# A two-layer hybrid encoder on one core: unused bytes between SBUF tiles that set the operands' addresses modulo 128

## The chip, the cores and the metric

One core of a Trainium2 chip. TensorE multiplies matrices (PE in the profile, and PEld for its loads of the operand that stays in the array), VectorE (DVE), ScalarE (ACT) and GpSimd (POOL) do the rest, SyncE (SP) issues most transfers. The metric is device time in microseconds of one execution. Three executions of the kernel before took 2242.03, 2242.40 and 2243.55 us; the median is 2242.4.

## The reference

Two layers over x of 256 tokens by 2048. Each layer:

```
h = x @ w_in                                   # 2048 -> 4928 columns
a = MLA heads (8, low-rank q and kv, rotary, chunk-causal softmax)
r = retention heads (4, decay, GroupNorm, swish gate)
x = LayerNorm(ALPHA * x + concat(a, r) @ w_out)
x = LayerNorm(ALPHA * x + (silu(x @ w_gate) * (x @ w_up)) @ w_down)   # 5632 wide
```

All in float32; nearly all of the work is products of x or of something made from x with weights that are read from memory once.

## The kernel before

A float32 product is made of three fp32r products: each operand is split into a high part (`split`, ACT writes `hi`) and a rest (DVE writes `lo`), and every 128 deep step of a product issues hi with hi, lo with hi, hi with lo. Weights come as units of up to 128 x 2048 numbers: SP loads one into a tile `raw`, ACT and DVE split it into `hi` and `lo` (three buffers of each), TensorE uses it, and `W.done()` lets the unit three further on be prepared. The order of all this is the order in which the Python code records it; tile pools decide the addresses.

A matmul instruction has a stationary operand of 128 columns, which PEld loads into the array, and a moving operand that streams through it. Two helpers issue nearly all of them. `mm_x` (lines 231 to 238) and `mm` of `strassen_group` (lines 790 to 795) keep 128 tokens of the activations still and stream 512 (once 320) weight columns. `mm_w` (lines 240 to 245) keeps 128 weight columns still and streams all 256 tokens. Every matmul loads a new stationary operand, so there are as many loads as matmuls.

The stages of a layer, with the tiles they write in PSUM: `cq` and `ckv` (`mm_x` over `xTh`, `xTl`), `pg` (`mm_w`), `pqn`, `pr`, `pkn`, `pv` (the low-rank q and kv, from `cqTh`, `cqTl` and `ckT`), `prv` with attention between it, `prq` (`mm_w`, retention), `wo` (over `mixAh`, `mixRh` and their `l`), then the feed-forward in four parts: `gb` and `ub` or, for ten of eleven column blocks, a Strassen group (`sX`, `sQ`, `sW`, `sY`, `sZ`, `sR` over `xTh`, `xTl`, and over four sums of it in `sfh`, `sfl`), and after each part `db` (`mm_x` over `hTh`, `hTl` with `w_down`).

Where the tiles lie, as the built program has it (first byte within a partition, modulo 128; every slice that a matmul takes begins at a multiple of 512 bytes in its tile): `res`, `xTh`, `xTl` at 0. `ident`, `raw`, `hi`, `lo` at 96, since the pool `const` ends 96 bytes past a multiple of 128. `sfh`, `sfl`, `hTh`, `hTl` and the Strassen blocks' own `raw` (pool `rs`) at 32. Attention tiles (`cqTh`, `mixAh`, `mixRh`, ...) at 64, because the table `cst` of 1953 numbers ends 32 bytes off; in layer 0 the slots `rg`, `rv`, `s8` are laid out ahead of `cst` and lie at 32, so `ckT` is at 32 in layer 0 and at 64 in layer 1.

So the two operands of a matmul lie 0, 32 or 64 bytes apart modulo 128 (the shorter way round):

| kind | moving over stationary | columns | matmuls | before: moving, stationary | apart | after | apart |
|---|---|---|---|---|---|---|---|
| a | `hi`, `lo` over `xTh`, `xTl` | 512 | 3600 | 96, 0 | 32 | 64, 0 | 64 |
| b | `hi`, `lo` over `mixA`, `mixR`, `cqT`; `ckT` of layer 1 | 512 | 840 | 96, 64 | 32 | 64, 0 | 64 |
| c | `xTh`, `xTl` over `hi`, `lo` (`pg`, `prq`) | 256 | 2304 | 0, 96 | 32 | 0, 64 | 64 |
| d | `cqT`; `ckT` of layer 1, over `hi`, `lo` (`pqn`, `pkn`) | 256 | 240 | 64, 96 | 32 | 0, 64 | 64 |
| e | `hi`, `lo` over `xTh`, `xTl` (`ckv`) | 320 | 192 | 96, 0 | 32 | 64, 0 | 64 |
| f | `hi`, `lo` over `hTh`, `hTl`, `sfh`, `sfl`; `ckT` of layer 0 | 512 | 3096 | 96, 32 | 64 | 64, 0 | 64 |
| g | `ckT` of layer 0 over `hi`, `lo` (`pkn`) | 256 | 48 | 32, 96 | 64 | 0, 64 | 64 |
| h | transposes: `ident` over `v`, `sf`, `sg` | 128 | 208 | 96, 32 | 64 | 96, 0 | 32 |
| i | transposes: `ident` over the rest | 128 | 252 | 96, 0 or 64 | 32 | 96, 0 | 32 |
| k | float32 products of attention and retention, two passes each | 128, 256 | 304 | several | 0 or 32 | 0, 0 | 0 |

These are the 11084 matmuls of the trace.

Of the kernel before, what the change touches and what calls it, by code (L numbers as in the profile page):

```python
# [10 lines left out]
F32 = mybir.dt.float32  # L11
# [7 lines left out]
P = 128  # L19
# [17 lines left out]

C_DEC, C_MASK, C_INVR, C_INVM = 0, HR * 384, HR * 384 + 384, HR * 384 + 385
N_CONST = C_INVM + RD // 2
N_COLS = 4 + 2 + 8 + 8  # L40


# [68 lines left out]
def trunk(ctx: ExitStack, tc: tile.TileContext, x, pos, w, lnp, cols, eye, consts, out):  # L111
    nc = tc.nc
    V, A, PE, G = nc.vector, nc.scalar, nc.tensor, nc.gpsimd

    const = ctx.enter_context(tc.tile_pool(name="const", bufs=1))
# [7 lines left out]
    xTl = const.tile([P, KD, S], F32R, name="xTl")  # L123
    colt = const.tile([P, DEPTH * N_COLS], F32, name="colt")
    rtC = const.tile([P, 1, S], F32, name="rtC")
# [3 lines left out]
    mhalf = const.tile([P, 8], F32, name="mhalf")  # L129

    ident = const.tile([P, P], F32, name="ident")

    def bank(tag_name):
        return psp.tile([P, 512], F32, tag="ps", name=tag_name)
# [96 lines left out]
    def mm_x(ps, ncol, tok, unit, xh, xl, k0, nk, first, last):  # L231
        wh, wl = unit
        for k in range(nk):
            sh = xh[:, k0 + k, tok * P:(tok + 1) * P]
            sl = xl[:, k0 + k, tok * P:(tok + 1) * P]
            PE.matmul(ps[:, :ncol], sh, wh[:, k, :ncol], start=first and k == 0, stop=False)  # L236
            PE.matmul(ps[:, :ncol], sh, wl[:, k, :ncol], start=False, stop=False)  # L237
            PE.matmul(ps[:, :ncol], sl, wh[:, k, :ncol], start=False, stop=last and k == nk - 1)  # L238
# [76 lines left out]
    def chunk_tail(banks, nu, xh, xl, k0, fin):  # L315
        for u in range(nu - 3):
            (unit,) = W.get()
            for tok in range(2):
                mm_x(banks[tok], 512, tok, unit, xh, xl, k0 + 4 * u, 4, u == 0, False)
            W.done()  # L320
        units = W.get(3)
        for i in range(3):
            u = nu - 3 + i
            mm_x(banks[0], 512, 0, units[i], xh, xl, k0 + 4 * u, 4, u == 0, u == nu - 1)
        fin(0)
        for i in range(3):
            u = nu - 3 + i
            mm_x(banks[1], 512, 1, units[i], xh, xl, k0 + 4 * u, 4, u == 0, u == nu - 1)
            W.done()
            if i < 2:  # L330
                pop(1)
        fin(1)

    def ln_params(pool, tags, i):
        g = pool.tile([P, D], F32, tag=tags[0], name=f"lng{i}")
        b = pool.tile([P, D], F32, tag=tags[1], name=f"lnb{i}")
        nc.sync.dma_start(g, lnp[2 * i].partition_broadcast(P))
        nc.sync.dma_start(b, lnp[2 * i + 1].partition_broadcast(P))
        return g, b
# [1 line left out]
    V.memset(mhalf, -0.5)  # L341

    def att_consts():
        cst = att.tile([P, N_CONST], F32, tag="cst", name="cst")
        nc.sync.dma_start(cst, consts)
        krE = att.tile([P, S], F32, tag="krE", name="krE")
        krO = att.tile([P, S], F32, tag="krO", name="krO")
        V.memset(krE, 0.0)
        V.memset(krO, 0.0)
        return cst, krE, krO  # L350

    att_ctx = ExitStack()
    att = att_ctx.enter_context(tc.tile_pool(name="att0", bufs=1))
# [18 lines left out]
    nc.scalar.dma_start(posc, pos.rearrange("(t p) -> p t", p=P))  # L372
    nc.sync.dma_start(posr, pos.partition_broadcast(P))
    cst, krE, krO = att_consts()
    nc.sync.dma_start(colt, cols)
    norm = Norm("i")
# [38 lines left out]
    for l in range(DEPTH):  # L415
        col = colt[:, l * N_COLS:(l + 1) * N_COLS]
        if l:
            att_ctx = ExitStack()
            att = att_ctx.enter_context(tc.tile_pool(name=f"att{l}", bufs=1))
            cst, krE, krO = att_consts()  # L420
# [262 lines left out]
        def resid(banks, c, t, norm_, scale=ALPHA):  # L683
            y = res[:, t, 512 * c:512 * (c + 1)]
            V.scalar_tensor_tensor(y, y, scale, banks[t], ALU.mult, ALU.add)  # L685
            if norm_ is not None:
                norm_.stat(t, c)
# [45 lines left out]
        ffp = ff_ctx.enter_context(tc.tile_pool(name=f"ff{l}", bufs=1))  # L733
# [23 lines left out]
        def h_flush(hTh, hTl, f0):  # L757
            while hprev:
                t, c, hh = hprev.pop(0)
                pt = bank("pth")  # L760
                for j in range(4):
                    PE.transpose(pt[:, j * P:(j + 1) * P], hh[:, j * P:(j + 1) * P], ident)
                k0 = 4 * (c - f0)
                split(hTh[:, k0:k0 + 4, t * P:(t + 1) * P], hTl[:, k0:k0 + 4, t * P:(t + 1) * P],
                      pt.rearrange("p (j t) -> p j t", j=4))
# [17 lines left out]
        def strassen_group(c, flush):  # L783
# [74 lines left out]
            hprev.append((0, c, v2))  # L858
            hprev.append((1, c, v5))

        for f0, f1 in FF_PARTS:
            nk = 4 * (f1 - f0)
            hTh = ffp.tile([P, 12, S], F32R, tag="hTh", name="hTh")
            hTl = ffp.tile([P, 12, S], F32R, tag="hTl", name="hTl")
            flush = lambda: h_flush(hTh, hTl, f0)
            for c in range(f0, f1):
                (strassen_group if c else plain_group)(c, flush)
            first, final = f0 == 0, f1 == NFF
            if final:
                g, b = ln_params(ffp, ("sfh", "sfl"), 2 + 2 * l)  # L870
            nu = f1 - f0
            for n in range(4):
                db = [bank(f"db{t}") for t in range(2)]
                if not final or n < 3:
                    for u in range(nu):
                        (unit,) = W.get()
                        for t in range(2):
                            mm_x(db[t], 512, t, unit, hTh, hTl, 4 * u, 4, u == 0, u == nu - 1)
                        W.done()
                        if u == nu - 2:  # L880
                            flush()
                    for t in range(2):
                        resid(db, n, t, normf if final else None, ALPHA if first else 1.0)
                else:
                    last = l == DEPTH - 1

                    def fin_f(t, db=db, g=g, b=b):
                        resid(db, 3, t, normf, 1.0)
                        normf.close(t)
                        if last:  # L890
                            for c in range(4):
                                normf.apply(t, c, g, b, transpose=False)
                                nc.sync.dma_start(out[t * P:(t + 1) * P, 512 * c:512 * (c + 1)],
                                                  res[:, t, 512 * c:512 * (c + 1)])
                        else:
                            for c in range(4):
                                pend.append(lambda c=c: normf.apply(t, c, g, b))

                    chunk_tail(db, nu, hTh, hTl, 0, fin_f)
# [29 lines left out]
def _consts():  # L929
    c = np.zeros((P, N_CONST), np.float32)  # L930
    m = np.arange(P)[:, None]
    n = np.arange(S)[None, :]
    for h in range(HR):
        lg = np.log1p(-2.0 ** (-5.0 - h))
        d = np.exp(lg * np.abs(n - m)) * (n // CHUNK >= m // CHUNK) / 16.0
        c[:, C_DEC + 384 * h:C_DEC + 384 * h + 256] = d
        c[:, C_DEC + 384 * h + 256:C_DEC + 384 * (h + 1)] = d[:, :P]
    q = np.arange(P)[:, None]
    for o, qb, nk in ((0, 0, 128), (128, 1, 256)):
        k = np.arange(nk)[None, :]  # L940
        c[:, C_MASK + o:C_MASK + o + nk] = np.where((q + qb * P) // CHUNK >= k // CHUNK, 0.0, -BIG)
    for dim, where in ((256, "r"), (RD, "m")):
        e = (-np.arange(0, dim, 2, dtype=np.float32) / np.float32(dim)).astype(np.float64)
        f = np.power(10000.0, e).astype(np.float32)
        if where == "r":
            c[:, C_INVR] = f
        else:
            c[:, C_INVM:C_INVM + 32] = f[None, :]
    return c
# [50 lines left out]
```

## Time and profile before

| | |
|---|---|
| median of three executions | 2242.4 us |
| profiled execution | 2244.0 us |
| its span, first to last instruction | 2242.2 us |
| busy in that span: PE, PEld | 2200.6, 1846.4 us |
| DVE, ACT, POOL | 1591.3, 1026.0, 35.5 us |
| granted TensorE clock, mean | 0.995 |
| memory read | 437.38 MB |

PE counts as busy from a matmul's start to its modelled end, and consecutive matmuls overlap (one of 512 columns is shown with some 395 ns, but the next starts well before that). What a matmul costs in a dense stretch is therefore the distance between two starts, read from the timeline: the time from the first start to the last, divided by one less than the count.

### The profile page before, as it was taken

What the parts mean: (1) busy time and instruction counts of PE and PEld (TensorE: products, weight loads), DVE (VectorE), ACT (ScalarE), POOL (GpSimd) and SP (SyncE); (2) the same over time, 40 slices, a digit from 0 to 9 for tenths busy, and PEclk for the clock granted to TensorE, in tenths of its full rate; (3) what the DMA queues carried; (4) which work ended last, traced back from release to release, by engine and by line L of the source; (5) the groups of instructions that cost most, each with busy time, mean ns of one, the idle gap of its engine ahead of it and who ended that gap; (6) DMA issues with size and microseconds to landing.
All of it is one profiled execution on the core that took longest, in us unless ns stands there. A gap on an engine that the chain in (4) does not pass through costs nothing. (4 is left out here: it accounts for less than half of the span.)

```text
span 2242.2 us, 26855 instructions
## 1 busy us (share of the span) xinstructions
PE 2200.6 (98%) x11084; PEld 1846.4 (82%) x11084; DVE 1591.3 (71%) x1687; ACT 1026.0 (46%) x1089; POOL 35.5 (2%) x46
## 2 busy tenths in 40 slices
PE   7999999899999999999999999999999999999998
PEld 5988988688888888888889899877888888888886
DVE  7565665787688578788675656766866885877976
ACT  3554333454455355455344533334544553544552
POOL 0000000000000000000000000000000000000000
PEclk9999999999999999999999999999999999999999
DMA  7544554566567556475555344545565764666653
GB/s 255 208 150 151 172 204 169 207 199 233 169 208 256 194 204 228 166 255 187 196 196 180 140 170 169 205 171 188 199 247 173 245 225 171 204 244 206 207 206 113
DMA packets 63467, 441.22 MB, mean 197 GB/s; under 512 B 7408, under 2 KB 7664, under 8 KB 11504
## 3 DMA queue, kind: packets, MB, share of 16 engines
q1 hardware_dynamic: 60048, 418.46, 51.2%
q0 software_dynamic: 2880, 20.97, 5.1%
q8 instruction: 87, 1.43, 0.3%
q14 instruction: 36, 0.29, 0.0%
q10 hardware_dynamic: 416, 0.07, 0.0%
HBM read 437.38 MB, written 2.10 MB: 196 GB/s over the span
## 5 line engine op out<-in xcount | busy, mean ns | idle before, releaser
L249 DVE TENSOR_TENSOR lo<-raw,hi 128x1024 fp32r<-128x1024 f32 (+3 forms) x754 | 1033.9, 1407 | 449.5 <-ACT hi L248 447.4
L248 ACT CAST hi<-raw 128x1024 fp32r<-128x1024 f32 (+3 forms) x754 | 875.2, 1199 | 1016.3 <-PE db L238 298.5
L236 PE MATMUL db<-hi,hTh 128*128 128x512 f32 x704 | 277.3, 394 | 0.0
L237 PE MATMUL db<-lo,hTh 128*128 128x512 f32 x704 | 276.8, 393 | 0.0
L238 PE MATMUL db<-hi,hTl 128*128 128x512 f32 x704 | 272.1, 390 | 0.0
L236 PEld LDWEIGHTS db<-hi,hTh 128*128 128x128 f32 x704 | 132.2, 188 | 32.7 <-ACT hTh L248 3.7
L238 PEld LDWEIGHTS db<-hi,hTl 128*128 128x128 f32 x704 | 132.2, 188 | 29.1
L237 PEld LDWEIGHTS db<-lo,hTh 128*128 128x128 f32 x704 | 132.4, 188 | 26.9
L243 PE MATMUL prq<-xTh,hi 128*128 128x256 f32 x512 | 144.7, 283 | 0.0
L244 PE MATMUL prq<-xTl,hi 128*128 128x256 f32 x512 | 143.1, 279 | 0.0
L245 PE MATMUL prq<-xTh,lo 128*128 128x256 f32 x512 | 142.6, 279 | 0.0
L185 DVE TENSOR_TENSOR raw<-raw,raw 128x2048 f32<-128x2048 f32 x60 | 137.2, 2286 | 0.5
L795 PE MATMUL sX<-hi,xTl 128*128 128x512 f32 x320 | 126.6, 395 | 0.0
L794 PE MATMUL sX<-lo,xTh 128*128 128x512 f32 x320 | 126.5, 395 | 0.0
L793 PE MATMUL sX<-hi,xTh 128*128 128x512 f32 x320 | 126.5, 395 | 0.0
L244 PEld LDWEIGHTS prq<-xTl,hi 128*128 128x128 f32 x512 | 96.3, 188 | 0.1
L243 PEld LDWEIGHTS prq<-xTh,hi 128*128 128x128 f32 x512 | 96.2, 188 | 0.1
L245 PEld LDWEIGHTS prq<-xTh,lo 128*128 128x128 f32 x512 | 96.2, 188 | 0.0
L795 PE MATMUL sQ<-hi,xTl 128*128 128x512 f32 x240 | 94.9, 395 | 0.0
L794 PE MATMUL sQ<-lo,xTh 128*128 128x512 f32 x240 | 94.9, 395 | 0.0
L793 PE MATMUL sQ<-hi,xTh 128*128 128x512 f32 x240 | 94.9, 395 | 0.0
L685 DVE SCALAR_TENSOR_TENSOR res<-res,db 128x512 f32<-128x512 f32 x64 | 43.8, 685 | 67.8 <-PE db L238 67.8
(265 smaller groups left out, 3998.2 us busy)
## 6 DMA issues: line engine op xcount, KB each, us to landing
raw<-w SPq DMA_DIRECT2D x377, 1024.0 KB, 4.9
raw<-w POOLq DMA_DIRECT2D x20, 1024.0 KB, 8.4
raw<-w SPq DMA_DIRECT2D x8, 640.0 KB, 3.8
lng<-lnp SPq DMA_DIRECT2D x4, 1024.0 KB, 4.8
lnb<-lnp SPq DMA_DIRECT2D x4, 1024.0 KB, 5.6
res<-x SPq DMA_DIRECT2D x4, 512.0 KB, 6.4
out<-res SPq DMA_DIRECT2D x8, 256.0 KB, 2.6
cst<-consts SPq DMA_DIRECT2D x2, 976.5 KB, 8.1
```

Of the source, the lines that this page charges most:

```text
L185: V.tensor_tensor(r[into], r[into], r[frm], ALU.add)
L236: PE.matmul(ps[:, :ncol], sh, wh[:, k, :ncol], start=first and k == 0, stop=False)
L237: PE.matmul(ps[:, :ncol], sh, wl[:, k, :ncol], start=False, stop=False)
L238: PE.matmul(ps[:, :ncol], sl, wh[:, k, :ncol], start=False, stop=last and k == nk - 1)
L243: PE.matmul(ps_ap, wh[:, k, c0:c0 + P], xh[:, k, :], start=k == 0, stop=False)
L244: PE.matmul(ps_ap, wh[:, k, c0:c0 + P], xl[:, k, :], start=False, stop=False)
L245: PE.matmul(ps_ap, wl[:, k, c0:c0 + P], xh[:, k, :], start=False, stop=k == nk - 1)
L248: A.copy(hi, src)
L249: V.tensor_tensor(lo, src, hi.bitcast(F32), ALU.subtract)
L793: PE.matmul(ps, a, wh[:, k, :], start=first and k == 0, stop=False, skip_group_check=True)
L794: PE.matmul(ps, a, wl[:, k, :], start=False, stop=False, skip_group_check=True)
L795: PE.matmul(ps, b, wh[:, k, :], start=False, stop=k == 3, skip_group_check=True)
```

## The change

A tile of 352 unused bytes per partition after `ident` moves the pools behind it (`raw`, `hi`, `lo`) from 96 to 64 modulo 128; `cst` gets 1984 columns in place of 1953 (the transfer fills the first 1953), so that all attention tiles lie at 0; and 384 unused bytes in the feed-forward's pool bring what lies behind them to 0. The table above has the places of all operands before and after. `ident` stays at 96.

```
--- before.py
+++ after.py
@@ -37,6 +37,7 @@
 
 C_DEC, C_MASK, C_INVR, C_INVM = 0, HR * 384, HR * 384 + 384, HR * 384 + 385
 N_CONST = C_INVM + RD // 2
+W_CONST = -(-N_CONST // 32) * 32
 N_COLS = 4 + 2 + 8 + 8
 
 
@@ -129,6 +130,7 @@
     mhalf = const.tile([P, 8], F32, name="mhalf")
 
     ident = const.tile([P, P], F32, name="ident")
+    const.tile([P, 88], F32, name="pad0")
 
     def bank(tag_name):
         return psp.tile([P, 512], F32, tag="ps", name=tag_name)
@@ -341,8 +343,8 @@
     V.memset(mhalf, -0.5)
 
     def att_consts():
-        cst = att.tile([P, N_CONST], F32, tag="cst", name="cst")
-        nc.sync.dma_start(cst, consts)
+        cst = att.tile([P, W_CONST], F32, tag="cst", name="cst")
+        nc.sync.dma_start(cst[:, :N_CONST], consts)
         krE = att.tile([P, S], F32, tag="krE", name="krE")
         krO = att.tile([P, S], F32, tag="krO", name="krO")
         V.memset(krE, 0.0)
@@ -858,6 +860,7 @@
             hprev.append((0, c, v2))
             hprev.append((1, c, v5))
 
+        ffp.tile([P, 96], F32, tag="pad", name="pad1")
         for f0, f1 in FF_PARTS:
             nk = 4 * (f1 - f0)
             hTh = ffp.tile([P, 12, S], F32R, tag="hTh", name="hTh")
```

The built programs hold the same instructions in the same order on all five engines; only addresses (and line numbers of the source, by one to three) differ.

## Rows read from the trace of the kernel before

**Rows 1.** The page, part 1: busy time, share of the span, instructions.

```profile
PE 2200.6 (98%) x11084; PEld 1846.4 (82%) x11084; DVE 1591.3 (71%) x1687; ACT 1026.0 (46%) x1089; POOL 35.5 (2%) x46
...
```

**Rows 2.** Waits of PE: engine, line <- releaser: us in total, times, longest.

```profile
PE ptx L280 <- DVE res L276: 16.3, 7, 11.3
PE pts L752 <- issue: 8.4, 2, 4.2
...
PE gb L236 <- ACT xTh L248: 1.4, 2, 0.7
```

**Rows 3.** Timeline of PE (start, us, what): `pkn`, layer 0, first and last of 48.

```profile
127.00 0.28 PE L243 MATMUL pkn<-ckT,hi 128*128 128x256 f32 x1
...
132.33 0.28 PE L245 MATMUL pkn<-ckT,lo 128*128 128x256 f32 x1
```

**Rows 4.** Timeline of PE: `pkn` of layer 1, first and last of 48.

```profile
1232.02 0.28 PE L243 MATMUL pkn<-ckT,hi 128*128 128x256 f32 x1
...
1237.65 0.28 PE L245 MATMUL pkn<-ckT,lo 128*128 128x256 f32 x1
```

**Rows 5.** Timeline of PE: `db` in part 1 of layer 0, second and last of 240.

```profile
552.40 0.40 PE L237 MATMUL db<-lo,hTh 128*128 128x512 f32 x1
...
607.06 0.40 PE L238 MATMUL db<-hi,hTl 128*128 128x512 f32 x1
```

**Rows 6.** Timeline of PE: Strassen block over `xT`, first and last of 60.

```profile
643.51 0.40 PE L793 MATMUL sW<-hi,xTh 128*128 128x512 f32 x1
...
657.27 0.39 PE L795 MATMUL sX<-hi,xTl 128*128 128x512 f32 x1
```

**Rows 7.** Timeline of PE: `sZ`, over `sfh` and `sfl`, first and last of 12.

```profile
672.30 0.39 PE L793 MATMUL sZ<-hi,sfh 128*128 128x512 f32 x1
...
674.82 0.40 PE L795 MATMUL sZ<-hi,sfl 128*128 128x512 f32 x1
```

**Rows 8.** Timeline of PE: `wo` over `mixRh` and on, layer 1, first and last of 270.

```profile
1433.03 0.48 PE L236 MATMUL wo<-hi,mixRh 128*128 128x512 f32 x1
...
1496.12 0.40 PE L238 MATMUL wo<-hi,mixRl 128*128 128x512 f32 x1
```

**Rows 9.** Timeline of PE: `pg` (second, last of 240) and `pqn` (first, last of 96).

```profile
81.99 0.28 PE L244 MATMUL pg<-xTl,hi 128*128 128x256 f32 x1
...
109.76 0.28 PE L245 MATMUL pg<-xTh,lo 128*128 128x256 f32 x1
109.87 0.28 PE L243 MATMUL pqn<-cqTh,hi 128*128 128x256 f32 x1
...
121.27 0.28 PE L245 MATMUL pqn<-cqTh,lo 128*128 128x256 f32 x1
```

**Rows 10.** Timeline of PE: `ckv` of layer 0, first and last of 96.

```profile
49.44 0.31 PE L236 MATMUL ckv<-hi,xTh 128*128 128x320 f32 x1
...
63.38 0.30 PE L238 MATMUL ckv<-hi,xTl 128*128 128x320 f32 x1
```

**Rows 11.** Chain that ended last (start us, us, what): transposes of `qo` and of `v`.

```profile
1237.93 0.87 PE pqr L554 x8
...
1657.20 0.87 PE pth L762 x8
```

**Rows 12.** Timeline of DVE: two block sums of a Strassen group.

```profile
611.80 2.29 DVE L185 TENSOR_TENSOR raw<-raw,raw 128x2048 f32<-128x2048 f32 x1
...
622.35 2.29 DVE L185 TENSOR_TENSOR raw<-raw,raw 128x2048 f32<-128x2048 f32 x1
```

**Rows 13.** Stretches: us, busy us of PE, PEld, DVE, ACT, POOL (count), PEclk, DMA share, GB/s.

```profile
60.00:130.00 70.00, 70.00 (x571) 68.91 (x570) 41.92 (x69) 37.03 (x55) 1.44 (x2) 1.00 0.57 196
429.80:433.30 3.50, 3.50 (x16) 3.06 (x15) 3.25 (x6) 1.97 (x4) 0.00 (x0) 0.51 0.95 403
440.00:540.00 100.00, 100.00 (x440) 81.05 (x439) 82.19 (x62) 52.28 (x45) 1.91 (x2) 1.00 0.62 212
1532.30:1539.20 6.90, 5.16 (x21) 4.76 (x22) 6.21 (x9) 2.42 (x5) 0.00 (x0) 0.51 0.79 304
```

More of the change, by code (lines that the diff above doesn't have):

```diff
@@ L39 @@
 N_CONST = C_INVM + RD // 2
+W_CONST = -(-N_CONST // 32) * 32
 N_COLS = 4 + 2 + 8 + 8
@@ L131, in trunk @@
     ident = const.tile([P, P], F32, name="ident")
+    const.tile([P, 88], F32, name="pad0")
     def bank(tag_name):
@@ L343, in att_consts @@
     def att_consts():
-        cst = att.tile([P, N_CONST], F32, tag="cst", name="cst")
-        nc.sync.dma_start(cst, consts)
+        cst = att.tile([P, W_CONST], F32, tag="cst", name="cst")
+        nc.sync.dma_start(cst[:, :N_CONST], consts)
         krE = att.tile([P, S], F32, tag="krE", name="krE")
@@ L859, in strassen_group @@
             hprev.append((1, c, v5))
+        ffp.tile([P, 96], F32, tag="pad", name="pad1")
         for f0, f1 in FF_PARTS:
```

## Prediction

> **What bounds the kernel now.** I read the page's first part, then the waits of PE, then the timeline of PE in stretches where nothing but one kind of matmul runs. PE is busy for 2200.6 of the span's 2242.2 us, DVE for 1591.3, ACT for 1026.0 [rows 1]. The waits that PE has are few: 16.3 us before the first transposes, 8.4 us before the transposes of the four sums `sf`, and a few of a microsecond or less at the heads of `cq` and `gb` [rows 2]. No wait on a weight unit in the middle of a layer stands in that view. So the kernel is a row of 11084 matmuls, and its time is their number by the distance between two starts. A saving of a nanosecond in each would be 11 us.
>
> That distance is not the same for equal instructions. The reader is to see it first in `pkn`: the same line, the same 48 matmuls, the same tiles, once in each layer. In layer 0 they take 127.00 to 132.33, which is 5.33 us over 47 distances or 113.4 ns [rows 3]; in layer 1 it is 1232.02 to 1237.65, 5.63 us or 119.8 ns [rows 4]. The granted clock is full around the first, 1.00 from 60 to 130 us [rows 13]. What differs is `ckT`'s place: at 32 modulo 128 in layer 0, 64 bytes from the weights at 96, and at 64 in layer 1, 32 bytes from them. The other stretches sort in the same way. With 512 columns: `db`, 64 apart, 552.40 to 607.06 over 238 distances, 229.7 ns [rows 5]; `sZ`, 64 apart, 2.52 us over 11, 229.1 ns [rows 7]; the neighbours of `sZ` over `xT`, 32 apart, 13.76 us over 59, 233.2 ns [rows 6]; `wo`, 32 apart, 63.09 us over 269, 234.5 ns [rows 8]. With 256 columns, all 32 apart: `pg` 27.77 us over 238, 116.7 ns, `pqn` 11.40 us over 95, 120.0 ns [rows 9]. `sW`, `sX` and `sZ` come from one helper, so the code does not explain their difference.
>
> A rule of the Trainium skill speaks against all this: "TensorE: Matmul & The Clock Gate", part 2, says that PE reads the moving operand and the weight load through two independent ports, so that loading the next weights takes nothing from the running matmul. By it no address matters, the sum below is 0 and the time stays at 2242. The trace of `pkn` does not agree: 119.8 against 113.4 ns [rows 3, 4].
>
> **The change part by part.** It removes and adds no instruction, moves none, and adds no wait; the unused tiles cost nothing, and the transfer of `cst` carries the same bytes. Only distances change. Kinds as in the table above; the price is the distance now, less that of the nearest stretch that is already 64 apart.
>
> - a, 3600 of 512 columns: 233.2 to between 229.7 (`db`, the longest stretch) and 229.1 (`sZ`, the nearest neighbour), so 3.5 to 4.1 ns; I take the middle, 3.8, since both forms occur: 13.7 us (12.6 to 14.8).
> - b, 840: 234.5 to the same two, 4.8 to 5.4 ns, taken 5.0: 4.2 us (4.0 to 4.5).
> - c, 2304 of 256 columns: 116.7 to the 113.4 of `pkn`, 3.3 ns: 7.6 us. Below, this could be nothing if the loads are the limit (a rival); above, 3.8 ns as in a, 8.8 us.
> - d, 240: 120.0 and 119.8 to 113.4, 6.5 ns: 1.6 us.
> - e, 192 of 320 columns: 13.94 us over 95 is 146.7 ns now [rows 10], and no stretch of this form is 64 apart. Between c and a, 3.3 to 3.8 ns: 0.7 us.
> - f and g, 3144: 64 apart before and after, taken as 0. Bounds: up by what `xT` costs more, or down by as much (two rivals).
> - h, 208 transposes go from 64 to 32 apart: at worst 4.1 ns each, 0.9 us. Eight transposes of `v`, 64 apart, take 0.87 us, and eight of `qo`, 32 apart, take 0.87 [rows 11]: 0.
> - i and k: i stays; in k, 56 of 304 passes move from 32 to 0 apart, at the 6.5 ns of d either way 0.4 us: 0.
>
> The sum is 27.8 us. Not all of it lies on the path: 384 matmuls of kind a are the heads `cq` and `gb`, where PE stops for `xT` [rows 2] and reaches the stop earlier instead. They hold 384 x 3.8 = 1.5 us; I take off half, 0.8. That leaves 27.0 us.
>
> The cover: DVE and ACT prepare each unit while PE works, and their tiles move as well. In the Strassen stage DVE is busy for 82.19 of 100 us [rows 13]; the same work in 1.2 us less (320 matmuls of kind a) is 83%, so it keeps up. Its speed should not change either: the block sum at 611.80 has both operands at 32, the one at 622.35 has one at 32 and one at 96, and both take 2.29 us [rows 12]. If that cover went, PE would wait in every Strassen group; nothing points there.
>
> One thing is chance: PE runs at half the clock, 0.51 and so 1.2 GHz, from 429.8 to 433.3 and from 1532.3 to 1539.2 us [rows 13], after the stops for `sf`. These stretches of 3.5 and 6.9 us cost half their length, 1.7 and 3.4 us, and each may come out like the other: 1.7 us either way.
>
> Sum against the profiled execution: 2244.0 - 27.0 = 2217.0 us. The median of the runs is 1.6 us lower, so the forecast for it is 2215 us. Its own range: the low bounds of a to e make 26.4 us, the high ones 30.4, the heads take 0 to 1.5, so the gain is 24.9 to 30.4 and the time 2212 to 2217.5; with up to 3.4 us of the clock either way, 2209 to 2221.
>
> **The rivals.**
>
> - *The place counts, not the distance* (slower). Every fast stretch has one operand at 32 modulo 128, and after the change no fp32r matmul has one there. Then the 3096 of kind f rise to at least the 233.2 of `xT`, 3.8 ns or 11.8 us, the 48 of g add 0.2, and a to e keep their time: 2242.4 + 12 = 2254. It is decided by whether `db` starts lie over or under 230 ns apart. Against it: in `db` the stationary operand is the one at 32, in `pkn` the moving one, with different partners in line and role; what they share is the 64 bytes. For it: 0 against 64 does not occur before. Chance 0.07.
> - *No address matters*: a running matmul and the next load do not meet, and the sorting has another cause in each stage: nothing is gained, 2242. The two `pkn` stretches speak against it. Chance 0.03. This is what the Trainium skill's page named above would make of the change.
> - *The loads bound the matmuls of 256 columns.* From 60 to 130 us PEld is busy for 68.91 of 70.00 us [rows 13], so c and d could be held by loads and keep their 9.2 us: 2215 + 9 = 2224. Against it `pkn` runs at 113.4 ns with as many loads. Chance 0.07.
> - *The even places are better still*: 0 and 64 beat 32 and 96, and f falls by as much as a, 3096 x 3.8 = 11.8 us: 2203. Chance 0.06.
> - *The cover tears*: a transfer, ACT or DVE is late in the Strassen groups and half of the gain is lost again, 2229. Chance 0.03.
>
> **How the numbers follow.** The forecast has 0.74. With most of the rival at 2224 in it, a range of 2208 to 2225 holds about 0.8; what it leaves out is the two ends, 2203 and 2242 to 2254. A measurement of this kernel can tell about 0.2%, 4.5 us, from no change. Faster by more than that: the forecast, the loads, the even places and the torn cover, 0.90, of which I give 0.01 to a cover torn so far that nothing is left: 0.89. Same: that 0.01 and the 0.03 in which no address matters, 0.04. Slower: 0.07.
>
> **What would show it.** In the trace after, `pkn` has one distance in both layers, near 113.4 ns; `sX` and the other blocks over `xT` come down from 233.2 to `sZ`'s 229 to 230; `wo` from 234.5 to the same; `pg` and `prq` from 116.7 to 113.4; `db` stays at 229.7; waits of PE, busy times of DVE and ACT, and bytes stay as they are. Wrong would be: `db` over 233 (the place counts), `pg` unmoved beside a faster `sX` (loads), or new waits of PE on `hi` or `lo`.

## The result, and the profile after

The change takes 2229.4 us (median, 2227.7 to 2230.7) against 2243.0 for the kernel before, measured beside it: a ratio of 0.9939, 95% interval 0.9922 to 0.9956. It is faster, by half of what was forecast (2215, range 2208 to 2225).

The page, part 1, and the waits of PE after (engine, line <- releaser: us in total, times, longest):

```profile
PE 2186.6 (98%) x11084; PEld 1839.3 (83%) x11084; DVE 1590.7 (71%) x1687; ACT 1025.6 (46%) x1089; POOL 35.5 (2%) x46
```

```profile
PE ptx L282 <- DVE res L278: 17.6, 7, 11.6
PE pts L754 <- issue: 8.4, 2, 4.2
...
PE gb L238 <- ACT xTh L250: 1.4, 2, 0.7
```

Nothing is new here: the waits of [rows 2] are there with 17.6 for 16.3 us and the same 8.4 and 1.4, DVE and ACT are busy for what they were in [rows 1]. The 14 us are gone from PE's busy time, 2186.6 for 2200.6. So it is the distances between starts, as forecast, and they are read from the timeline (start us, us, what). First what answers to [rows 8], `wo` over `mixRh` and on, from the second row to the last of 270, and to [rows 4], `pkn` of layer 1, first and last of 48:

```profile
1423.82 0.39 PE L239 MATMUL wo<-lo,mixRh 128*128 128x512 f32 x1
...
1485.16 0.39 PE L240 MATMUL wo<-hi,mixRl 128*128 128x512 f32 x1
```

```profile
1225.25 0.28 PE L245 MATMUL pkn<-ckT,hi 128*128 128x256 f32 x1
...
1230.61 0.28 PE L247 MATMUL pkn<-ckT,lo 128*128 128x256 f32 x1
```

`wo`: 61.34 us over 268 distances, 228.9 ns, from 234.5 (from 234.2 without the first distance of [rows 8], which is a longer one). `pkn`: 5.36 over 47, 114.0, from 119.8. Both as forecast. Then `pg` in two stretches, second and last of 96 and of 240, for [rows 9]:

```profile
63.65 0.28 PE L246 MATMUL pg<-xTl,hi 128*128 128x256 f32 x1
...
74.72 0.28 PE L247 MATMUL pg<-xTh,lo 128*128 128x256 f32 x1
...
82.15 0.28 PE L246 MATMUL pg<-xTl,hi 128*128 128x256 f32 x1
...
109.13 0.28 PE L247 MATMUL pg<-xTh,lo 128*128 128x256 f32 x1
```

11.07 us over 94 is 117.8 ns, and 26.98 over 238 is 113.4: the same code, the same tiles, two values in one run. `ckv` ([rows 10]) did not move at all:

```profile
49.44 0.31 PE L238 MATMUL ckv<-hi,xTh 128*128 128x320 f32 x1
...
63.38 0.31 PE L240 MATMUL ckv<-hi,xTl 128*128 128x320 f32 x1
```

And `db` ([rows 5]), second and last of 240, with the blocks over `xT` behind it ([rows 6]): 60 of the next Strassen group, and 60 of the group after that:

```profile
545.15 0.40 PE L239 MATMUL db<-lo,hTh 128*128 128x512 f32 x1
...
600.79 0.40 PE L240 MATMUL db<-hi,hTl 128*128 128x512 f32 x1
...
637.42 0.40 PE L795 MATMUL sW<-hi,xTh 128*128 128x512 f32 x1
...
651.19 0.40 PE L797 MATMUL sX<-hi,xTl 128*128 128x512 f32 x1
...
679.78 0.39 PE L795 MATMUL sW<-hi,xTh 128*128 128x512 f32 x1
...
693.28 0.40 PE L797 MATMUL sX<-hi,xTl 128*128 128x512 f32 x1
```

`db` went up, from 229.7 to 55.64 over 238, 233.8 ns, with its distance of 64 modulo 128 unchanged. The first Strassen group behind it stays slow as well, 13.77 over 59, 233.4; the next one is at 13.50 over 59, 228.8. Added up over the trace, from each start to the next, the kinds of the table changed by:

| kind | before, us | after, us | change | forecast |
|---|---|---|---|---|
| a | 868.9 | 856.3 | -12.6 | -13.7, less 0.8 at the heads |
| b | 198.2 | 194.0 | -4.2 | -4.2 |
| c | 271.9 | 267.5 | -4.4 | -7.6 |
| d | 28.8 | 27.2 | -1.6 | -1.6 |
| e | 28.2 | 28.2 | 0.0 | -0.7 |
| f | 713.3 | 722.0 | +8.7 | 0 |
| g, h, i, k | 110.3 | 110.6 | +0.3 | 0 |

That is -13.8 us; the span fell by 13.3.

### The profile page after: what moved, and what is told of

Same layout as the page of the kernel before. It is cut to its first block, busy times and chain, and to the rows that moved or that the text cites. A ratio compares the mean times of both kernels' runs of the same rounds, so it can differ in the third digit from the quotient of the medians.

```text
span 2228.9 us, 26855 instructions
## 1 busy us (share of the span) xinstructions
PE 2186.6 (98%) x11084; PEld 1839.3 (83%) x11084; DVE 1590.7 (71%) x1687; ACT 1025.6 (46%) x1089; POOL 35.5 (2%) x46
## 4 chain that ended last, share of the span: by engine, by line
PE 96%; DVE 2%; issue 1%; ACT 0%; DMA 0%; DVEq 0%; ACTq 0%
PE db L238 7%; PE db L240 7%; PE db L239 7%; PE sX L797 3%; PE sW L797 3%; PE sX L796 3%; PE sX L795 3%; PE sW L796 3%; PE sW L795 3%; PE prq L246 3%; PE prq L245 3%; PE prq L247 3%; PE wo L239 3%; PE wo L238 3%; PE sQ L797 2%; PE wo L240 2%
## 5 line engine op out<-in xcount | busy, mean ns | idle before, releaser
L187 DVE TENSOR_TENSOR raw<-raw,raw 128x2048 f32<-128x2048 f32 x60 | 137.1, 2285 | 0.5
```

Source lines behind the costliest of these rows:

```text
L187: V.tensor_tensor(r[into], r[into], r[frm], ALU.add)
```

## The experiments

D is from here on the place of the weight tile (`hi`, `lo`) less that of the activation tile, modulo 512, whichever of the two moves. The change gives `xT` and `sf` D = 64, `mix` and `cqT` 320, and `hT` 192. In the kernel before, `xT` had 224, `sf` 64, `mix` and `cqT` 416, and `hT` 64. For the distance modulo 128, 64 and 192 are the same thing; modulo 256 they are 64 bytes in opposite directions. Distances given as one number for a kind are means over the whole trace without those more than 12 ns over the median (stops); for `xT` with 512 columns they are taken over the Strassen blocks.

**e1_no_pad1**: the change without the pad ahead of `hTh`.

```diff
-        ffp.tile([P, 96], F32, tag="pad", name="pad1")
```

> The change without the 384 unused bytes ahead of hTh. D is the place of the weight tile less that of the activation tile, modulo 512. hT goes from D = 192 back to 64; all other tiles stay where the change has them. Theory 'direction' (the weights 64 bytes ahead, D = 64 modulo 256, are fast, and 64 bytes behind, D = 192, are slow): db falls from 233.4 to some 229.2 ns, 2112 x 4.2 = 8.9 us, so 2229.4 - 8.9 = 2220.5 us. Theory 'distance modulo 128' (that of the prediction, with db slow for another reason): 384 is a multiple of 128, nothing changes, 2229 us.

Measured: 2221.6 us (2219.8 to 2223.8), ratio to before 0.9902 (0.9886 to 0.9919). `db`, second and last of 240:

```profile
547.74 0.40 PE L239 MATMUL db<-lo,hTh 128*128 128x512 f32 x1
...
602.38 0.39 PE L240 MATMUL db<-hi,hTl 128*128 128x512 f32 x1
```

54.64 over 238, 229.6 ns: back where it was. The Strassen blocks over `xT` are at 228.9 on average (230.05 in the change, where some groups are slow). The distance modulo 128 falls as a theory, since 384 bytes are three times 128.

**e5_pad1_only**: the kernel before with that pad alone.

```diff
+        ffp.tile([P, 96], F32, tag="pad", name="pad1")
         for f0, f1 in FF_PARTS:
```

> The kernel before with the 384 bytes ahead of hTh alone. Only hT moves, from D = 64 to 192; its distance modulo 128 stays 64. Theory 'direction': db rises from 229.1 to some 233.4 ns, 2112 x 4.3 = 9.1 us, 2243.0 + 9 = 2252 us. Theory 'distance modulo 128': same, 2243 us. Theory 'both at multiples of 64 are slow for hT': same too, since weights lie at 96 here.

Measured: 2251.7 us (2251.0 to 2253.0), ratio 1.0040 (1.0025 to 1.0055), slower. `db`, second and last of 240:

```profile
553.41 0.39 PE L237 MATMUL db<-lo,hTh 128*128 128x512 f32 x1
...
609.07 0.40 PE L238 MATMUL db<-hi,hTl 128*128 128x512 f32 x1
```

55.66 over 238, 233.9 ns, with the weights at 96 modulo 128 here and at 64 in the change: this one pad costs 8.6 us here, and 7.8 us in the change (2229.4 less e1's 2221.6).

**e2_pad0_96**: the kernel before with 96 bytes after `ident`.

```diff
     ident = const.tile([P, P], F32, name="ident")
+    const.tile([P, 24], F32, name="pad0")
```

> The kernel before with 96 unused bytes after ident and nothing else: weights and all attention and feed-forward tiles move by 96 together, only xTh and xTl stay. D is unchanged for hT and sf (64) and for mix and cqT (416); for xT it goes from 224 to 320. mix now lies at 32 modulo 256, the place at which hT was fast before. Theory 'direction': wo stays at 234.2 ns, db at 229.1, the Strassen blocks over xT fall to 229 to 230, pg and prq to 113.4 to 115.1; gain 3600 x 3.2 to 4 plus 2304 x 1.9 to 3.3, 16 to 22 us, some 2224 us. Theory 'place' (what counts is where the activation tile lies): wo falls to 229 as well, 768 x 5 = 3.8 us more, some 2220 us.

Measured: 2222.4 us (2221.3 to 2222.8), ratio 0.9907 (0.9893 to 0.9922). `wo`, second and last of 270, and `db`, second and last of 240:

```profile
1417.34 0.39 PE L238 MATMUL wo<-lo,mixRh 128*128 128x512 f32 x1
...
1480.13 0.39 PE L239 MATMUL wo<-hi,mixRl 128*128 128x512 f32 x1
```

```profile
545.73 0.40 PE L238 MATMUL db<-lo,hTh 128*128 128x512 f32 x1
...
600.37 0.39 PE L239 MATMUL db<-hi,hTl 128*128 128x512 f32 x1
```

`wo` 62.79 over 268, 234.3 ns: as slow as before, although `mix` now lies at 32 modulo 256, where `hT` was fast. `db` 54.64 over 238, 229.6, although both its tiles have moved. `xT`, which alone changed its D (224 to 320), fell to 228.9. So it is the difference that counts, and the rival of the place falls. One pad of 96 bytes does as much as e1's two edits, within what can be measured.

**s1, s2, s4**: sweeps of D, with tiles of unused bytes and a wider `cst` at different sizes, and small constant tiles moved ahead of `xTh`. The edit of s1 against the change, cut to the lines that differ (the others have other numbers; s2 moves only `colt`, s4 has a pad after `ident` and a larger `pad1` too):

```diff
-W_CONST = -(-N_CONST // 32) * 32
+W_CONST = 2040
...
+    colt = const.tile([P, DEPTH * N_COLS], F32, name="colt")
+    mhalf = const.tile([P, 8], F32, name="mhalf")
     xTh = const.tile([P, KD, S], F32R, name="xTh")
     xTl = const.tile([P, KD, S], F32R, name="xTl")
-    colt = const.tile([P, DEPTH * N_COLS], F32, name="colt")
...
-    mhalf = const.tile([P, 8], F32, name="mhalf")
...
-    const.tile([P, 88], F32, name="pad0")
...
+        ffp.tile([P, 112], F32, tag="padf", name="padf")
         sfh = ffp.tile([P, 4, 4, P], F32R, tag="sfh", name="sfh")
```

> Places that no run has had: D is 0 for xT, 96 for mix and cqT, 128 for sf, 256 for hT (small constant tiles laid ahead of xTh, a wider cst, pads ahead of sfh and hTh). Theory 'direction, period 256': hT at 256 costs what xT at 0 costs. Theory 'direction, period 512': they may differ. What 0, 96 and 128 cost no theory says; if the cost falls off around 64 on both sides evenly, 96 is near 231 and 0 and 128 near 233 ns.

> A sweep: D is 32 for xT, 128 for mix and cqT, 160 for sf, 288 (32 modulo 256) for hT. By 'direction, period 256' hT at 288 costs what xT at 32 costs with 512 columns, between the 227 of D = 0 and the 229 of 64; mix at 128 costs the 232.9 of sf in s1, and sf at 160 the 234.2 of wo before. With 256 columns, pg and prq at 32 fall between 120 (D = 0) and 113 to 118 (64).

> A sweep: D is 128 for xT, 0 for mix and cqT, 480 (224 modulo 256) for sf, 32 for hT. By 'direction, period 256' mix falls to 227, sf rises to 233.2 as xT had at 224 before, hT costs what it costs at 288 in s2, and xT costs the 232.9 of sf in s1 at 128. By 'direction, period 512' hT and sf may differ from these.

One run each: 2229.2, 2256.2 and 2249.6 us beside some 2243 for the kernel before. s1, Strassen blocks over `xT` (D = 0), first and last of 60, and `pg` (D = 0), second and last of 240:

```profile
641.20 0.40 PE L795 MATMUL sW<-hi,xTh 128*128 128x512 f32 x1
...
654.60 0.40 PE L797 MATMUL sX<-hi,xTl 128*128 128x512 f32 x1
```

```profile
80.70 0.28 PE L245 MATMUL pg<-xTl,hi 128*128 128x256 f32 x1
...
109.25 0.28 PE L246 MATMUL pg<-xTh,lo 128*128 128x256 f32 x1
```

13.40 over 59 is 227.1 ns, the lowest yet with 512 columns; 28.55 over 238 is 120.0, as high as `pqn` in [rows 9]. With all runs together (where a cell has two levels, see after_again below):

| D modulo 256 | 512 columns, ns (tile, kernel) | 256 columns, ns |
|---|---|---|
| 0 | 227.1 (`hT`, s1), 227.3 (`mix`, s4), 227.7 (`xT`, s1) | 119.9 (`xT`, s1), 119.9 (`cqT`, s4) |
| 32 | 233.3 (`xT`, s2), 233.3 (`hT`, s2 and s4) | 118.3 (`xT`, s2) |
| 64 | 228.9 (`xT`, e1), 229.1 (`hT`, e1), 229.0 (`mix`, e1); up to 233.3 | 113.3 or 117.8 (`xT`, the change) |
| 96 | 233.3 (`mix`, s1) | 117.4 (`cqT`, s1) |
| 128 | 232.9 (`sf`, s1), 232.4 (`mix`, s2), 232.3 (`xT`, s4) | 118.9 (`xT`, s4) |
| 160 | 234.2 (`mix`, before), 233.4 (`sf`, s2) | 120.0 (`cqT`, before) |
| 192 | 233.4 (`hT`, the change), 233.3 (`mix`, m1) | 117.8 (`cqT`, m1) |
| 224 | 233.2 (`xT`, before), 232.7 (`sf`, s4) | 116.7 or 117.8 (`xT`, before) |

`hT` at 288 costs what `xT` and `hT` cost at 32; `mix` at 320 what `hT` costs at 64: the period is 256, not 512, to within 0.8 ns. With 512 columns only 0 and 64 are fast of the eight places tried, which lie 32 bytes apart. That the cost would fall off evenly around 64, a guess in s1's expectation, is wrong: 32 is slow and 0 is the best. With 256 columns the order is another, and 0 is among the worst.

**b1**: D = 0 modulo 256 for `sf`, `hT` and `mix`, which matter with 512 columns, and 64 for `xT`, which is used with both. The edit against the change, cut to the lines that differ:

```diff
-W_CONST = -(-N_CONST // 32) * 32
+W_CONST = 2000
...
+        ffp.tile([P, 16], F32, tag="padf", name="padf")
         sfh = ffp.tile([P, 4, 4, P], F32R, tag="sfh", name="sfh")
...
-        ffp.tile([P, 96], F32, tag="pad", name="pad1")
```

> The change without the pad ahead of hTh, with 64 unused bytes ahead of sfh, and cst wider by 64 bytes more: D stays 64 for xT, and becomes 0 modulo 256 for sf, hT and mix, the place at which s1 had 227.0 to 227.7 ns with 512 columns. Theory 'direction, period 256': hT 2112 x 2.0, sf 960 x 1.5, mix 768 x 2.0 = 7.2 us under e1_no_pad1, less 192 + 48 matmuls of 256 columns over cqT and ckT that go to D = 0 (120 ns in s1, against some 115 to 118), 0.7 us: 2221.6 - 6.5 = 2215 us. If D = 64 were the best place and s1's 227 had another cause (xT at 0 as well, no change of place within a Strassen group), hT and sf stay near 229 and the time at 2221 us.

Measured: 2212.9 us (2212.0 to 2213.9), ratio 0.9865 (0.9848 to 0.9881): the fastest, 30 us under the kernel before and 16 under the change. `db`, second and last of 240:

```profile
545.02 0.40 PE L239 MATMUL db<-lo,hTh 128*128 128x512 f32 x1
...
599.22 0.39 PE L240 MATMUL db<-hi,hTl 128*128 128x512 f32 x1
```

54.20 over 238, 227.7 ns. Over the trace `hT` is at 226.9, `sf` at 226.8, `mix` at 227.3, `pqn` at 119.8.

**m1**: as b1, but `hTl` alone 64 bytes later (D = 192 modulo 256, `hTh` at 0), and `mix` and `cqT` at 192 (to make room, `colt` lies ahead of `xTh` and the pad after `ident` is smaller, which leaves `xT` at 64). Of its edit, the lines on `hTl`:

```diff
             hTh = ffp.tile([P, 12, S], F32R, tag="hTh", name="hTh")
+            ffp.tile([P, 16], F32, tag="padl", name="padl")
             hTl = ffp.tile([P, 12, S], F32R, tag="hTl", name="hTl")
```

> As b1 (xT at D = 64, sf at 0), but hTl alone 64 bytes later, so that hTh keeps D = 0 and hTl has 192, and cst wider, so that mix, cqT and ckT of layer 1 have D = 192. In db the steps are hi over hTh, lo over hTh, hi over hTl. If a stream collides with the load of the next stationary operand, only the step lo over hTh (during which hTl is loaded) can cost more: one step of three near 233 to 240 ns and the other two near 227. If it collides with what its own stationary operand's place does, the step hi over hTl costs more. If one bad pair puts the whole chain into the slow pattern, all three steps are near 233. wo at 192: 233.4 as db had in the change. pqn at 192, which 256 columns never had: between 113 and 120, 113 or 118 if 64 in either direction is good for this form.

One run: 2224.4 us. In `db` the distance from hi over `hTh` to the next start is 228.6 ns, from lo over `hTh` 229.6, from hi over `hTl` 235.1; in b1, where all three have D = 0, they are 226.9, 226.7 and 227.1. In the timeline, which rounds to 10 ns, it shows as the step after each `hTl`:

```profile
570.28 0.39 PE L239 MATMUL db<-lo,hTh 128*128 128x512 f32 x1
570.51 0.40 PE L240 MATMUL db<-hi,hTl 128*128 128x512 f32 x1
570.75 0.39 PE L238 MATMUL db<-hi,hTh 128*128 128x512 f32 x1
570.98 0.39 PE L239 MATMUL db<-lo,hTh 128*128 128x512 f32 x1
571.20 0.40 PE L240 MATMUL db<-hi,hTl 128*128 128x512 f32 x1
571.44 0.39 PE L238 MATMUL db<-hi,hTh 128*128 128x512 f32 x1
```

By the recorded starts the bad pair costs most, 8.0 ns, while `hTl` is the matmul's own stationary operand, and not while it is being loaded in the step before. That is nearest to the second of the three outcomes in the expectation, though the two steps over `hTh` rose as well, by 1.7 and 2.9 ns, which none of the three foresaw. Whether a start is stamped a step early, which would turn this round, no run here tells.

**after_again**: the change itself, once more.

> The change itself once more, for a second trace. If the two distances of pg, prq and pkn at D = 64 (113.3 and 117.8 ns) are settled anew in every execution, the stretches that are fast will be others than in the first trace; if they follow from addresses or from the order of the work, they will be the same stretches. Time 2229 us either way.

One run: 2231.3 us. With 256 columns all stretches of `pg`, `pqn`, `pkn` and `prq` came out as in the first trace, fast where they were fast (54 pieces of 48 matmuls, each mean within 0.1 ns of the first). With 512 columns they did not. The end of the Strassen group that ran slow behind `db` in the first trace, first and last of the same 60:

```profile
637.07 0.39 PE L795 MATMUL sW<-hi,xTh 128*128 128x512 f32 x1
...
650.57 0.40 PE L797 MATMUL sX<-hi,xTl 128*128 128x512 f32 x1
```

13.50 over 59 is 228.8 ns, for 233.4 in the first trace, on the same tiles at the same places. Of the six Strassen groups that come straight behind a `db`, four were slow in the first trace and two in this one, only one of them in both. So with 256 columns the pattern was that of the program in these two executions, and with 512 it was in part that of the execution. Yet e1, which up to the first feed-forward has the same tiles at the same places, has another one. `pqn`, first and last of 96, in the change and in e1:

```profile
109.24 0.28 PE L245 MATMUL pqn<-cqTh,hi 128*128 128x256 f32 x1
...
120.01 0.28 PE L247 MATMUL pqn<-cqTh,lo 128*128 128x256 f32 x1
```

```profile
109.92 0.28 PE L245 MATMUL pqn<-cqTh,hi 128*128 128x256 f32 x1
...
121.11 0.28 PE L247 MATMUL pqn<-cqTh,lo 128*128 128x256 f32 x1
```

10.77 over 95, 113.4 ns, against 11.19, 117.8. What chooses the level at D = 64 stays open, for either column count.

## Why the prediction was wrong

- *PE bounds, and its distance depends on where the operands lie*: right. PE's busy time fell by 14.0 us, the span by 13.3, and one pad moves the time by 8.6 us without an instruction more or less (e5). The rule of the Trainium skill that I weighed ("TensorE: Matmul & The Clock Gate", part 2, two independent ports, so that the next load takes nothing from the running matmul) would have given 2242; the runs do not agree with it, since a pad alone moved the time from 2243.1 to 2251.7 us (e5). Why the difference modulo 256 matters, no run here shows.
- *Kinds a, b and d*: right in sum, 18.4 us measured, 18.7 forecast with the heads taken off, but in part by luck. In a, the Strassen blocks gave 8.3 us and not the 11.3 that they gave in e1, since some groups stayed slow behind `db`; `ub` gave 2.3 us, of which 4.3 ns on 192 matmuls make 0.8; the rest is the half clock, whose stretches reached into `ub` before (to 433.3 and 1539.2 us, [rows 13]) and hardly after. In d, the 1.6 us hang on the lower level: in e1, with the same tiles at the same D, d gave 0.5.
- *"f and g, 3144: 64 apart before and after, taken as 0"*: this step failed, by 8.7 us, and it is most of the miss. Its premise was that the distance modulo 128 decides. It is the signed distance modulo 256. `hT` went from 64 to 192, from 229.1 to 233.4 ns over 2112 matmuls; `sf` stayed at 64 and at 229.9. The upper bound of that step (what `xT` costs more) was right, but it hung on the rival of the place, which e2 excludes. There was a sign of it in the diff: the pad ahead of `hTh` is 384 bytes, three times 128, and does nothing by the theory on which I priced everything else. I did not ask what it was for.
- *Part c, 3.3 ns from `pkn` of layer 0*: mis-sized, 4.4 us measured for 7.6. With 256 columns D = 64 has two levels, 113.3 and 117.8 ns; `pkn` of layer 0 stood at the lower one in the kernel before, and one stretch of 48 could not show the other. `ckT` of layer 0 has D = 64 in all eleven traces, and that same `pkn` ran at 113.5 to 114.0 in seven of them and at 117.8 to 117.9 in four (e1, e2, s4, b1). So rows 3 and 4, on which I leant most, compared the lucky level of one place with another place: the conclusion stood, the size did not.
- *Part e, 0.7 us*: nothing, 146.6 to 146.7 ns in every kernel. With 320 columns the slices of a unit lie 1280 bytes apart, not a multiple of 512 as was said of all slices, so D alternates by 256, which is a whole period; that this form shows no dependence at all was not explained.
- *The cover, the transposes, kind k, the clock*: right. No new waits; DVE's 60 block sums take 137.1 us in all, 2.29 each as in [rows 12]; and the stretch at half clock, 6.9 us from 1532.3 in [rows 13], came out shorter, which the forecast had allowed for. In the table of stretches (us, busy us of PE, PEld, DVE, ACT, POOL with counts, PEclk, DMA share, GB/s) the 30 us around it after have a mean clock of 0.94, and 0.06 x 30 over the half that is lost makes 3.6 us:

```profile
440.00:540.00 100.00, 100.00 (x446) 82.17 (x445) 84.18 (x65) 53.38 (x47) 1.91 (x2) 1.00 0.65 217
...
1515.00:1545.00 30.00, 25.82 (x116) 21.41 (x115) 17.51 (x18) 13.05 (x15) 0.57 (x1) 0.94 0.49 184
```

The first row is the Strassen stage, where DVE is busy for 84.18 of 100 us and PE does not wait.
- *The rivals*: none as it stood. Two of the signs named for them did appear, `db` over 233 ns (the place) and a stretch of `pg` that did not come down (the loads); but `wo` and the blocks over `xT` did come down, and most of `pg` reached 113.4. "The even places are better still" came nearest for the wrong reason: with 512 columns there is a faster place than 64, D = 0, but the change has no tile there.

Without the pad ahead of `hTh` the time is 2221.6 us. That is inside the range that I gave, but still 6.6 over the forecast of 2215, mostly for parts c, d and e: the gains there were 2.4, 0.5 and 0 us.

## What to carry to other kernels

When PE streams back to back, look at the starts of equal matmuls on different tiles: they differed here by up to 3% with 512 columns and 6% with 256, and unused bytes alone took 1.3% off the time (b1). In these kernels the difference of the two operands' addresses modulo 256, with its sign, was the thing to sweep, for each pair of tiles and each column count by itself. A contrast of two stretches found in one trace fixes neither the variable nor the size: list the addresses to more bits than the theory needs, and look for a pair that the theory calls equal. And an edit in the diff that does nothing by your theory is evidence against the theory.

## What the runs showed of the hardware that I had not expected

With fp32r operands of 128 stationary and 512 moving columns, the distance between starts is 226.8 to 227.7 ns for D = 0 and 228.9 to 229.1 for D = 64 modulo 256 (233.3 where a stretch is slow), and 232.3 to 234.2 at the other six places tried. With 256 columns it is 113.3 or 117.8 ns at 64 and up to 120.0 at 0 and 160. A slow pattern can outlive its place: in the change four of the six Strassen groups behind the slow `db` ran at 233.3 to 233.4 ns on tiles at D = 64 until the next transposes interrupted the stream, and at 228.8 after them. It does not always: two groups were fast from the start, and in the kernel before `sf`, at D = 64, ran at 229 to 230 ns straight behind slow blocks over `xT`. With 256 columns the level of each stretch was the same in two executions of one program, and another in a program that differs only later; with 512 columns it also differed between the two executions.
